# The low-part product of an attention logit, over 64 rows or over 128

## The chip, the cores and the metric

The kernel runs on one core of a Trainium2 chip. The metric is the device time of one execution in microseconds. Three runs of the kernel before took 2187.93, 2191.03 and 2192.39 us; their median, 2191.03 us, is the number that the prediction starts from.

## The reference, cut to what matters

The program is two transformer blocks, one after the other, on 512 tokens of width 1024, all in float32. Two places of it hold the products that the change touches: the selecting attention of the first block, with its scores and its logits, and the second attention of the second block.

```python
def dsa_attention(q, k, v, q_idx, k_idx, w_idx):     # first block, 4 blocks of 128 queries
    def block(args):
        raw = jnp.einsum('bqhd,bsd->bqhs', qib, k_idx) * idx_scale            # 8 heads of 64
        score = jnp.einsum('bqhs,bqh->bqs', jax.nn.relu(raw), wb)
        score = jnp.where(causal[None], score, -jnp.inf)
        _, sel = lax.top_k(score, k_top)                                      # 128 keys
        logits = jnp.einsum('bqhd,bqkd->bqhk', qb, k_sel) * attn_scale        # 8 heads of 64
        p = jax.nn.softmax(logits, axis=-1)
        return jnp.einsum('bqhk,bqkd->bqhd', p, v_sel)

def blocked_attention(q, k, v):                      # second block, 8 heads of 64, 2 of keys
    def one_block(qblk):
        s = jnp.einsum("bqhgd,bkhd->bhgqk", qblk, k)
        pr = jax.nn.softmax(s, axis=-1)
        return jnp.einsum("bhgqk,bkhd->bqhgd", pr, v)
```

## The kernel before, in words

Activations lie with features on partitions and tokens in the free dimension, 512 to a tile. TensorE takes float32r operands. So that products come out with float32 accuracy, each operand is a pair of tiles, a high part and a low part whose sum is the value, and a product of weights and activations is three matmuls (`mm3`, L283 to L285: high by high, high by low, low by high). Most of the program is streams of such products: for each output tile of 128 features a DMA brings 512 KB of weights, ScalarE casts the high part (L246), VectorE subtracts to get the low part (L247), and 24 matmuls of 512 columns follow.

The logits with heads of 64 features are made in another way, by `logits` (L629 to L636). A head has 64 rows only, so its tile of queries `q` (made in `heads`) holds the high part in 64 rows and the low part in the other 64. Keys (made in `keys`) come as two tiles: `hh` holds the high part in both halves of the rows, `ll` holds the low part in both halves. The first matmul (L635) multiplies all 128 rows of `q` with `hh`, which gives high by high plus low by high. The second (L636) multiplies the 64 rows of `q` with the high part by the 64 rows of `ll` beside them, which adds high by low, in the same bank of PSUM.

`logits` is called 88 times, at three places:

- **Scoring**, in `mix` (L790): 24 calls, 8 heads for each of three blocks of queries, with 256, 384 and 512 keys. ScalarE takes the result out of PSUM with a ReLU (L792), VectorE multiplies and adds it to the block's scores (L793). Then VectorE selects the best 128 keys of each query with 16 rounds of a maximum and a replacement (L804, L805), while TensorE goes on with the projections of the convolution's branch.
- **First attention**, in `mix` through `group` (L698): 32 calls, with 256 keys (16), 384 (8) and 512 (8). VectorE adds the bias and takes the maximum (L645), ScalarE exponentiates, VectorE scales.
- **Second attention**, in `mix2` through `group`: 32 calls with 512 keys. VectorE takes the maximum (L648).

In both attentions the weights of a group of four heads are transposed on TensorE (L670), split by ScalarE and VectorE (L672, L673), and multiplied with the values (L684, L685), one group behind the logits; products of the gates' weights stand between. The logits have three banks of PSUM ("lg"). Each engine works through its own list of instructions in order; the lists are made by the framework's scheduler from the order of the program and its own estimates.

Of the kernel before, what the change touches and what calls it, by code (L numbers as in the profile page):

```python
# [19 lines left out]
P = 128  # L20
# [18 lines left out]
# Columns of the array of per-feature vectors.  # L39
# [10 lines left out]
# Output tiles of w_in, in the order in which they are used.  # L50
T_KK, T_QI, T_VW, T_QA, T_CONV, T_GB, T_GA = 0, 1, 5, 6, 10, 22, 30
# Output tiles of w_in_2.
# [6 lines left out]
# How the work is cut and shared between the engines: P for GpSimd, V for VectorE, A for ScalarE.  # L59
# [116 lines left out]
class Net:  # L176
    def __init__(self, ctx, tc, a):
        self.tc, self.nc, self.a = tc, tc.nc, a
        pool = lambda name, bufs, **k: ctx.enter_context(tc.tile_pool(name=name, bufs=bufs, **k))  # noqa: E731
        self.cp = pool("cp", 1)  # L180
        self.xp = pool("xp", 16)
        self.slots = {t: pool(t + "p", n) for t, n in SLOTS.items()}
        self.sp = pool("sp", 2)
        self.wr = pool("wr", 2)
        self.wh = pool("wh", 5)
        self.wl = pool("wl", 5)
        # PSUM by use, so that each use goes on when another has to wait.
        self.banks = {t: pool(t, n, space=PSUM) for t, n in BANKS.items()}
        self.turn = 0
        self.attending = False  # L190
        self.spared = False
        self.sums = 0
        self.n = 0
        # What is still to be done before the stream h can be read: the rest of the last products,
        # and a post-norm's tiles and gain.
        self.rest = []
        self.due = None
        # The engine that takes the second parts of weights.
        self.second = self.nc.vector
        # The same for those between phases.  # L200
        self.lead = self.nc.vector

    # ---- tiles
# [22 lines left out]
    def pm(self):  # L226
        """For products; those of the attention's logits too while there are none."""
# [7 lines left out]
    # ---- products: each operand is a pair of float32r parts whose sum is the float32 value  # L235
    def load(self, src, shape):
        """The parts of weights; src and shape are [128, ...]."""
# [6 lines left out]
        view = lambda t: t.rearrange(f"p ({names}) -> p {names}", **{f"d{i}": v for i, v in enumerate(shape[1:])})  # noqa: E731  # L244
# [5 lines left out]
    def weights(self, w, n, nk, k0=0, count=1):  # L250
        """For each of count output tiles from n, the parts of its k-tiles."""
# [7 lines left out]
    def lead_weights(self, w, n, nk, k0=0, tag="b"):  # L259
        """The same for one output tile, in tiles that are free between phases."""  # L260
# [3 lines left out]
        # At the start the stream's input comes between the parts.  # L264
# [22 lines left out]
    def lin(self, wt, xs, tok=ALL, bank=None):  # L287
        """One output tile [128 features, tokens]."""
# [5 lines left out]
    def begin(self, jobs, step, fill=()):  # L294
        """The products of jobs by halves of the tokens, after the rest of the last phase's and after
        fill, with the steps of each half's norms between the products of the other half."""
# [24 lines left out]
        # A product is taken once its half's norm is there.  # L321
# [16 lines left out]
    def stream(self, jobs, tail=0, spare=0):  # L338
        """jobs: (weights, output tile, parts of the k-tiles, first k-tile, what takes the product).
        Of the last, the second half of the tokens is left to the next phase; some of these have weights in  # L340
        tiles of the norm's input that are free by then."""
# [9 lines left out]
    def split(self, src, parts, scale=None):  # L351
        """Writes the parts of src, or of src times a value per partition."""
# [14 lines left out]
    # ---- norms  # L367
# [6 lines left out]
    def rsqrt(self, v, tag, bufs=2):  # L374
        """x ** -0.5 of a small tile that has v = ROOT * x: from the exponent's bits, then by an iteration
        of the third order and one of the second, whose factors 1.5 and 2.25 are in ROOT."""
# [21 lines left out]
    def _sumsq(self, srcs, tag="sh"):  # L398
        """Tiles whose sum has, per partition and token, the sum of the squares of srcs."""
# [11 lines left out]
        # Sums of a few; the last goes into the product with ones at once.  # L411
# [9 lines left out]
    def rstd(self, accs, size, tag="r", bufs=4):  # L421
        """(mean + eps) ** -0.5, tokens on partitions: [128, tokens / 128]."""
# [11 lines left out]
    def row(self, r):  # L434
        """A value per token on every partition, in PSUM: [128, tokens]."""
# [6 lines left out]
    def rows(self, r, out):  # L442
        """The same in out."""
        self.nc.scalar.copy(out, self.row(r))
        return out
# [4 lines left out]
    def enter(self, gain, more=None):  # L450
        """The parts of h times the gain, the norm's factor per token for what is made of them, and
        the steps that compute both for a half of the tokens, after the post-norm that is due."""
# [44 lines left out]
    def leave(self, f, gain):  # L497
        """h += norm(f) * gain, when h is next needed."""
        self.due = f, gain

    # ---- parts of the net
    def setup(self):
        nc, a = self.nc, self.a
        c = lambda name, shape, dt=F32: self.cp.tile(shape, dt, tag=name, name=name)  # noqa: E731
# [4 lines left out]
        # The first activation brings the table of functions of the first part.  # L509
# [7 lines left out]
        # The stream's input, between the first weights.  # L517
# [5 lines left out]
        # The gains of the post-norms that the reference multiplies by a half.  # L523
# [12 lines left out]
    def down(self, w, f, k0, xs, add, late=(0, 0)):  # L536
        """f (+)= the product with the k-tiles of w from k0."""
# [47 lines left out]
    def rotated(self, w, n, xs, cos, sin, g=None, squares=None):  # L585
        """A job, and the tile that gets rope(its product, times a gain per row where there is one)."""
# [3 lines left out]
        def put(ps, tok):  # L590
            if squares is not None:
                nc.scalar.activation(squares[:, tok], ps, AF.Square)
            # y takes the 32-row blocks of each 64 rows exchanged.
# [12 lines left out]
    def heads(self, x):  # L606
        """Two heads of 64 rows: for each a tile with its hi part in its own rows, its lo part in the other's."""
# [10 lines left out]
    def keys(self, x, e):  # L618
        """The parts of the keys in rows 64e.. of x, each in both halves of a tile."""
# [9 lines left out]
    def logits(self, ps, q, e, i, keys, n):  # L629
        """[128 queries, n keys] of the head in tile q, whose hi part is in rows 64e.."""  # L630
        mm = self.nc.tensor.matmul
        own = slice(64 * e, 64 * e + 64)
# [3 lines left out]
        mm(ps[:, :n], lhsT=q[own, qs], rhs=ll[own, :n], start=False, stop=True)  # L636

    def softmax(self, ps, scale, n, bias=None, pool="V"):
        """Weights over n keys, for a scale that is positive (a number or a value per query)."""
# [24 lines left out]
    def turned(self, ps_, j):  # L664
        """The parts of the transposes of block j of the weights of some queries, side by side."""
# [10 lines left out]
    def pv(self, ps_, v):  # L676
        """sum over j of v[j].T @ (block j of the weights).T; v[j] has its hi part in columns 0-63,
        its lo part in the others."""
# [11 lines left out]
    def group(self, i, g, q, keys, v, ot, n, soft):  # L690
        """Four heads that share keys and values, for the queries of tile i, in two steps."""
        nc = self.nc
        ps = []
        for j in range(4):
            hd = 4 * g + j
            l = self.bank("lg")
            # Fewer than 256 columns would take longer.
# [10 lines left out]
    def overlapped(self, units):  # L708
        """Pairs of a generator of two steps and other work, each first step and the work before the
        second step of the unit before."""  # L710
# [12 lines left out]
    def values(self, ps, n):  # L723
        """[128 keys, hi | lo] of values whose transposes are in the columns of ps."""
# [6 lines left out]
    def projection(self, w, n, xs, r, alloc=None, light=False):  # L731
        """A job, and the tile that gets its product times r: on GpSimd where VectorE has much to do."""
# [18 lines left out]
    def mix(self):  # L751
# [28 lines left out]
        # The indexer's scores, and a bias that leaves each query its best keys.  # L780
# [28 lines left out]
        # The convolution's branch.  # L809
# [21 lines left out]
        # The attention, beside the other branch's gates.  # L831
# [26 lines left out]
    def gates(self, w, n, xs, r, count):  # L858
        """Tiles that get tanh(g / 2) of the gates g in some output tiles, one for each step of the
        generator; sigmoid(g) is (1 + tanh(g / 2)) / 2."""  # L860
# [25 lines left out]
    def branch(self, gates, w, xs, done=None):  # L886
        """gates = (gates + 1) * product of w and xs."""
# [7 lines left out]
    def merge(self, ga, gb, w, xb):  # L895
        """The parts of half the sum of ga and (gb + 1) * product of w and xb."""
# [9 lines left out]
    def memory_parts(self):  # L906
        """The parts of the normalised memory."""
# [12 lines left out]
    def memory(self):  # L920
        """Keys [features, M] by head, and values [M, features], of the memory, and what computes them."""
# [55 lines left out]
    def mix2(self):  # L977
# [19 lines left out]
        # The latents: the queries' norm factor goes into the softmax's scale.  # L997
# [11 lines left out]
        # The rotated part of the keys, in rows 64-95 of the tiles of keys.  # L1009
# [11 lines left out]
        # The first attention. Its values have keys on partitions, [hi | lo] of each head.  # L1021
# [21 lines left out]
        def prepare(hd):  # L1043
            """The parts of the queries of heads hd and hd + 1, and their keys and values."""
            # The first ones come before there are logits.
            bank = lambda: self.bank(K["pr"] if hd else "lg")
            if hd % 4 == 0:
                if hd == 0:
                    va.append(first_values(0))
                # The rotated parts of four heads: output tiles of them, and of the same exchanged.  # L1050
# [23 lines left out]
        # The second attention's heads: keys and queries without the norm's factor per token, which is  # L1074
        # in what their own norms' factors are.
        r2 = self.small("rsq", [P, NT], 1)
        nc.vector.scalar_tensor_tensor(r2, rt, 1.0 / 64, rt, op0=OP.mult, op1=OP.mult)
        wide = lambda t: t.unsqueeze(2).to_broadcast([P, NT, 2])  # noqa: E731
        two = lambda t: t.rearrange("p (t e) -> p t e", e=2)  # noqa: E731
# [95 lines left out]
    def mlp(self):  # L1175
# [14 lines left out]
        # The stream takes each part's product; the norm's input is kept in xs and r.  # L1190
# [43 lines left out]
    def final(self):  # L1234
# [3 lines left out]
        def step(tok):  # L1238
# [8 lines left out]
            def rows():  # L1247
                n = width(tok)
                outs = [self.tmp((P, 2 * n)).rearrange("p (k t) -> p k t", k=2) for _ in range(KD // 2)]
                # GpSimd takes some, whose gain ScalarE multiplies by before the norm's factor is there.  # L1250
# [45 lines left out]
# ---- layout of the inputs  # L1296
# [126 lines left out]
```

## Time and profile before

| | |
|---|---|
| runs | 2187.93, 2191.03, 2192.39 us (median 2191.03) |
| profiled execution, span of its instructions | 2187.6 us |
| TensorE matmuls, busy | 2125.2 us, 97% |
| TensorE weight loads, busy | 1754.7 us, 80% |
| VectorE, busy | 1290.8 us, 59% |
| ScalarE, busy | 910.1 us, 42% |
| GpSimd, busy | 307.5 us, 14% |
| granted clock of TensorE, mean | 0.984 of full |

The page gives no time for the profiled execution beside its span. The span is 0.3 us under the shortest of the three runs and 3.4 us under their median. A matmul's record is longer than what it costs: matmuls overlap, and their ends are modelled. What one costs is therefore read from the distance between the starts of neighbours, not from the length of a record. The granted clock is a share of 2.4 GHz; 0.5 is 1.2 GHz. In rows with "[x <-y]", the engine stood idle for x us before the instruction, and y ended that.

### The profile page before, as it was taken

The page shows a single profiled execution, that of the slowest core. Times are in us where ns is not written, and L with a number is a line of the kernel's source. Part 1 is how long each engine was busy: PE and PEld are TensorE (multiplying, and loading weights), DVE is VectorE, ACT ScalarE, POOL GpSimd, SP SyncE. Part 2 cuts the span into 40 slices and gives each one's busy share as a digit, 9 for nine tenths or more (in the row PEclk, how much of TensorE's full clock was granted, in tenths as well). Part 3 has the DMA queues.
Part 4 walks back from the last instruction along what each step waited for, and adds up shares of the span by engine and source line. Part 5 has one row for each costly group of instructions (what it writes and reads, how often), then busy time and mean ns, then how long its engine had stood idle before and what let it go on. Part 6 is the DMA issues. An engine that isn't in the chain of part 4 may idle for free.

```text
span 2187.6 us, 27792 instructions
## 1 busy us (share of the span) xinstructions
PE 2125.2 (97%) x10718; PEld 1754.7 (80%) x10718; DVE 1290.8 (59%) x2427; ACT 910.1 (42%) x1603; POOL 307.5 (14%) x275
## 2 busy tenths in 40 slices
PE   8999999899999989999999999998999999999997
PEld 7788888868777888898888888876667898888887
DVE  6344344869874685574243447678977663443565
ACT  5232223654464454452322224466764332222352
POOL 1101012303332120041010013122110000000011
PEclk9999999989999999999999999999999999999998
DMA  5233333203213234212333332211012322333331
GB/s 158 89 101 97 93 91 101 76 21 100 93 47 108 78 100 132 87 59 83 101 92 91 97 107 83 68 45 48 30 48 78 110 74 90 95 96 96 104 99 39
DMA packets 60229, 186.15 MB, mean 85 GB/s; under 512 B 6337, under 2 KB 13505, under 8 KB 60097
## 3 DMA queue, kind: packets, MB, share of 16 engines
q1 hardware_dynamic: 57616, 180.97, 27.1%
q10 hardware_dynamic: 2448, 3.41, 0.5%
q8 instruction: 84, 1.38, 0.3%
q14 instruction: 49, 0.39, 0.1%
q0 software_dynamic: 32, 0.00, 0.0%
HBM read 182.25 MB, written 2.10 MB: 84 GB/s over the span
## 4 chain that ended last, share of the span: by engine, by line
PE 84%; DVE 7%; issue 3%; ACT 2%; POOL 2%; DMA 2%; SPq 0%; POOLq 0%; ACTq 0%; DVEq 0%
PE mm L284 15%; PE mm L283 15%; PE mm L285 15%; PE lg L283 11%; PE lg L285 11%; PE lg L284 11%; DVE h L476 2%; PE lg L636 2%; PE tt L670 1%; PE lg L635 1%; DVE wl L247 1%; PE o L685 1%; PE o L684 1%; PE tt L428 1%; ACT wh L246 1%
## 5 line engine op out<-in xcount | busy, mean ns | idle before, releaser
L246 ACT CAST wh<-wr 128x1024 fp32r<-128x1024 f32 (+3 forms) x314 | 325.7, 1037 | 761.0 <-PE lg L284 344.8
L247 DVE TENSOR_TENSOR wl<-wr,wh 128x1024 fp32r<-128x1024 f32 (+2 forms) x312 | 415.9, 1333 | 150.2 <-ACT wh L246 146.9
L283 PE MATMUL mm<-x,wh 128*128 128x512 f32 (+1 forms) x1080 | 420.2, 389 | 0.0
L284 PE MATMUL mm<-x,wh 128*128 128x512 f32 (+1 forms) x1080 | 418.9, 388 | 0.0
L285 PE MATMUL mm<-x,wl 128*128 128x512 f32 (+1 forms) x1080 | 417.9, 387 | 0.0
L283 PEld LDWEIGHTS mm<-x,wh 128*128 128x128 f32 x1080 | 204.2, 189 | 46.0 <-issue 2.7
L284 PEld LDWEIGHTS mm<-x,wh 128*128 128x128 f32 x1080 | 204.3, 189 | 44.2 <-issue 2.4
L285 PEld LDWEIGHTS mm<-x,wl 128*128 128x128 f32 x1080 | 204.1, 189 | 44.2 <-issue 1.6
L283 PE MATMUL lg<-x,wh 128*128 128x512 f32 (+1 forms) x624 | 233.2, 374 | 0.0
L285 PE MATMUL lg<-x,wl 128*128 128x512 f32 (+1 forms) x624 | 233.2, 374 | 0.0
L284 PE MATMUL lg<-x,wh 128*128 128x512 f32 (+1 forms) x624 | 233.1, 374 | 0.0
L283 PE MATMUL mm<-b,wh 128*128 128x512 f32 (+1 forms) x493 | 175.6, 356 | 0.1
L284 PE MATMUL mm<-b,wh 128*128 128x512 f32 (+1 forms) x493 | 174.8, 355 | 0.4 <-DVE b L357 0.2
L285 PE MATMUL mm<-b,wl 128*128 128x512 f32 (+1 forms) x493 | 174.7, 354 | 0.0
L283 PE MATMUL lg<-b,wh 128*128 128x512 f32 (+1 forms) x455 | 161.8, 356 | 0.0
L285 PE MATMUL lg<-b,wl 128*128 128x512 f32 (+1 forms) x455 | 161.4, 355 | 0.0
L284 PE MATMUL lg<-b,wh 128*128 128x512 f32 (+1 forms) x455 | 161.3, 355 | 0.0
L565 POOL TENSOR_TENSOR t<-t,t 128x512 f32<-128x512 f32 (+1 forms) x48 | 66.3, 1382 | 579.5 <-ACT wh L246 486.7
L283 PEld LDWEIGHTS lg<-x,wh 128*128 128x128 f32 x624 | 117.6, 189 | 22.7
L285 PEld LDWEIGHTS lg<-x,wl 128*128 128x128 f32 x624 | 117.5, 188 | 22.7
L284 PEld LDWEIGHTS lg<-x,wh 128*128 128x128 f32 x624 | 117.6, 188 | 22.6
L356 ACT CAST b<-t 128x512 fp32r<-128x512 f32 (+1 forms) x100 | 58.8, 588 | 141.1 <-POOL t L565 68.0
(297 smaller groups left out, 3619.1 us busy)
## 6 DMA issues: line engine op xcount, KB each, us to landing
wr<-in_ffn_w SPq DMA_DIRECT2D x110, 512.0 KB, 3.6
wr<-in_w_in SPq DMA_DIRECT2D x64, 512.0 KB, 3.6
wr<-in_w_up SPq DMA_DIRECT2D x32, 512.0 KB, 3.6
wr<-in_w_down SPq DMA_DIRECT2D x32, 512.0 KB, 3.9
wr<-in_ffn_w SPq DMA_DIRECT2D x16, 448.0 KB, 3.4
wr<-in_w_out SPq DMA_DIRECT2D x8, 512.0 KB, 3.5
wr<-in_xattn_w_k SPq DMA_DIRECT2D x8, 512.0 KB, 3.7
wr<-in_xattn_w_v SPq DMA_DIRECT2D x8, 512.0 KB, 3.8
```

Source lines behind the costliest of these rows:

```text
L246: nc.scalar.copy(hi, raw)
L247: self.second.tensor_tensor(lo, raw, hi.bitcast(F32), op=OP.subtract)
L283: mm(ps, lhsT=a[0], rhs=b[0], start=first, stop=False)
L284: mm(ps, lhsT=a[0], rhs=b[1], start=False, stop=False)
L285: mm(ps, lhsT=a[1], rhs=b[0], start=False, stop=last)
L356: nc.scalar.copy(hi, src)
L428: nc.tensor.matmul(ps[:, i : i + 1], lhsT=acc[:, i * P : (i + 1) * P], rhs=self.ones, start=j == 0, stop=j == len(accs) - 1)
L476: nc.vector.scalar_tensor_tensor(h[k][:, tok], f, self.g(due[1], k), h[k][:, tok], op0=OP.mult, op1=OP.add)
L565: nc.gpsimd.tensor_tensor(t3[:, tok], t3[:, tok], t1[:, tok], op=OP.mult)
L635: mm(ps[:, :n], lhsT=q[:, qs], rhs=hh[:, :n], start=True, stop=False)
L636: mm(ps[:, :n], lhsT=q[own, qs], rhs=ll[own, :n], start=False, stop=True)
L670: nc.tensor.transpose(ps[:, b * P : b * P + P], p[:, j * P : j * P + P], self.ident)
```

## The change

The second matmul of `logits` takes all 128 rows of `q` and of `ll`. It thereby adds the product of the low parts, which the kernel before leaves out, and it addresses all rows of the array instead of the upper or the lower half.

```diff
     def logits(self, ps, q, e, i, keys, n):
         mm = self.nc.tensor.matmul
-        own = slice(64 * e, 64 * e + 64)
         qs = slice(i * P, i * P + P)
         hh, ll = keys
         mm(ps[:, :n], lhsT=q[:, qs], rhs=hh[:, :n], start=True, stop=False)
-        mm(ps[:, :n], lhsT=q[own, qs], rhs=ll[own, :n], start=False, stop=True)
+        mm(ps[:, :n], lhsT=q[:, qs], rhs=ll[:, :n], start=False, stop=True)
```

Nothing else of the program differs but comments. Both halves of `ll` and of `q` are written in the kernel before as well. The lists of the five engines hold the same instructions in the same order with the same waits; line numbers from `logits` on are one lower.

## Rows read from the trace of the kernel before

**Rows 1.** The page: span, and busy time of TensorE.

```profile
span 2187.6 us, 27792 instructions
PE 2125.2 (97%) x10718; PEld 1754.7 (80%) x10718; DVE 1290.8 (59%) x2427; ACT 910.1 (42%) x1603; POOL 307.5 (14%) x275
```

**Rows 2.** The chain that ended last, by engine.

```profile
PE 84%; DVE 7%; issue 3%; ACT 2%; POOL 2%; DMA 2%; SPq 0%; POOLq 0%; ACTq 0%; DVEq 0%
```

**Rows 3.** All instructions of L636: loads, matmuls, idle time before them (us, times).

```profile
L636 PEld LDWEIGHTS lg<-b,b x88: 182/183/286, 441.5 to 1643.1; 64*128 64x128 f32 x88
L636 PE MATMUL lg<-b,b x88: 378/492/687, 441.5 to 1643.1; 64*128 64x512 f32 x48, 64*128 64x256 f32 x24, 64*128 64x384 f32 x16
...
  issue: 20.9, 75
```

**Rows 4.** Timeline of TensorE's matmuls, second attention (start us, length us, instruction).

```profile
1612.41 0.39 PE L283 MATMUL mm<-x,wh 128*128 128x512 f32 x1
1612.64 0.40 PE L284 MATMUL mm<-x,wh 128*128 128x512 f32 x1
...
1617.16 0.40 PE L635 MATMUL lg<-b,b 128*128 128x512 f32 x1
1617.49 0.50 PE L636 MATMUL lg<-b,b 64*128 64x512 f32 x1
1617.91 0.51 PE L685 MATMUL o<-u,v 128*128 128x512 f32 x1
1618.26 0.60 PE L670 MATMUL tt<-ident,t 128*128 128x128 f32 x4
```

**Rows 5.** Timeline of TensorE's weight loads, the same stretch.

```profile
1612.41 0.19 PEld L284 LDWEIGHTS mm<-x,wh 128*128 128x128 f32 x1
...
1617.48 0.18 PEld L636 LDWEIGHTS lg<-b,b 64*128 64x128 f32 x1 [0.36 <-issue]
```

**Rows 6.** Timeline of matmuls, first attention: four pairs of 256 keys.

```profile
588.05 0.28 PE L635 MATMUL lg<-b,b 128*128 128x256 f32 x1
...
590.45 0.50 PE L283 MATMUL mm<-x,wh 128*128 128x512 f32 x1
```

**Rows 7.** Timeline of matmuls: products over 96 rows, in the second block's other attention.

```profile
1536.87 0.40 PE L284 MATMUL lg<-b,b 96*128 96x512 f32 x1
1537.11 0.40 PE L285 MATMUL lg<-b,b 96*128 96x512 f32 x1
```

**Rows 8.** Timeline of matmuls, scoring: the first, two in its midst, and the first behind it.

```profile
441.16 0.39 PE L635 MATMUL lg<-b,b 128*128 128x256 f32 x1 [2.86 <-DVE b L614]
...
446.55 0.63 PE L285 MATMUL mm<-x,wl 128*128 128x512 f32 x1
446.98 0.63 PE L283 MATMUL mm<-x,wh 128*128 128x512 f32 x1
...
474.14 0.50 PE L283 MATMUL mm<-x,wh 128*128 128x512 f32 x1
```

**Rows 9.** Stretches: length; busy us of PE, PEld, DVE, ACT, POOL; PEclk; DMA.

```profile
393.80:397.20 3.40, 3.34 (x15) 3.35 (x16) 3.40 (x9) 2.43 (x7) 0.00 (x0) 0.51 0.42 139
441.60:462.10 20.50, 20.50 (x46) 12.56 (x46) 11.19 (x25) 7.93 (x20) 0.00 (x0) 0.50 0.09 26
462.10:474.10 12.00, 12.00 (x34) 5.70 (x32) 8.46 (x17) 7.36 (x13) 0.00 (x0) 1.00 0.00 0
474.10:578.80 104.70, 104.70 (x450) 84.51 (x450) 98.28 (x191) 45.77 (x66) 34.68 (x23) 1.00 0.29 88
580.00:643.00 63.00, 62.80 (x264) 43.91 (x263) 42.80 (x171) 40.34 (x94) 17.87 (x14) 1.00 0.17 51
1541.00:1643.20 102.20, 100.73 (x444) 69.75 (x443) 85.72 (x230) 72.39 (x139) 11.12 (x8) 1.00 0.12 37
```

**Rows 10.** ScalarE's ReLUs of scoring: shortest, median, longest (ns).

```profile
L792 ACT ACTIVATE t<-lg x24: 383/490/601, 445.4 to 474.2; 128x256 f32<-128x256 f32 x8, 128x384 f32<-128x384 f32 x8, 128x512 f32<-128x512 f32 x8
```

**Rows 11.** VectorE's longest wait in 1541 to 1643.2 (us, times, longest).

```profile
DVE u L673 <- ACT u L672: 7.0, 12, 1.3
```

## The prediction

> **What bounds the kernel now.** I read the page first. TensorE has matmuls under way in 2125.2 us of the span of 2187.6 us, and the chain that ended last runs over it for 84% [rows 1, 2]. So time that TensorE gains comes off the end, wherever no other engine is close behind it. But a busy share says nothing of whether the matmuls stand as close as they could. So I went to the line that changes, L636 [rows 3]: 88 matmuls, 48 of 512 columns, 24 of 256 and 16 of 384. Their weight loads have an idle time before them, 20.9 us in 75 cases, which is put down to "issue": they wait for nothing that the profile shows.
>
> The timeline tells what that is. A product of 512 columns over all rows starts 0.23 us after the one before it (1612.41 to 1612.64). From L635 to L636 it is 0.33 us (1617.16 to 1617.49), from L636 to the next matmul 0.42 (to 1617.91), and from that to its successor still 0.35 (to 1618.26) [rows 4]. The loads show why: the load for a product over all rows runs beside the matmul before it (L284's load starts at 1612.41, its matmul at 1612.64), while L636's load has waited 0.36 us and starts only with its own matmul [rows 4, 5]. My reading: TensorE lets everything run out when it goes from all rows to half of them, and again on the way back.
>
> Is it the number of rows, or that L636 adds to a bank and closes it? The other attention has triples of products that also add up in one bank, over 96 rows. They stand 0.24 us apart [rows 7]. So 96 rows count as a full array, and adding up costs nothing.
>
> Then I asked of each stretch who is next behind TensorE [rows 9]. In the first attention VectorE is busy 42.80 of 63.00 us and ScalarE 40.34: much room. In the second, VectorE is busy 85.72 of 102.20 us: little. In scoring the granted clock is 0.50 from 441.6 to 462.1, that is 1.2 GHz. Ahead of it TensorE had stood 2.86 us for VectorE [rows 8]. Behind scoring comes the selection, in which VectorE is busy 98.28 of 104.70 us [rows 9].
>
> **The change part by part.** Nothing is moved on any queue, and no wait is added. What changes is what 88 pairs cost.
>
> *One product.* The three distances in the second attention add up to 1618.26 - 1617.16 = 1.10 us; three plain ones are 3 x 0.233 = 0.70 (0.233 is the 0.23 of rows 4 over many products). Gain: 0.40 us. In the first attention four pairs of 256 columns take 590.45 - 588.05 = 2.40 us [rows 6] where eight plain products of half the columns take 8 x 0.117 = 0.94; with 0.10 for the product behind them as in rows 4, the gain is (2.40 - 0.94 + 0.10) / 4 = 0.39 us. The width hardly matters, so I take 0.40 us everywhere at full clock. What the 64 further rows may cost: a load takes 183 ns over 64 rows and 0.19 us over 128 [rows 3, 5], and both lie beside a matmul. I cost it at nothing; without that cover it is 88 x 7 ns = 0.6 us.
>
> *First attention:* 32 x 0.40 = 12.8 us. VectorE and ScalarE leave 20 us of room, so all of it counts. Lower bound 10, if a fifth goes to waits for results.
>
> *Second attention:* 32 x 0.40 = 12.8 us. VectorE's work with its longest wait, for ScalarE's split of the transposed weights [rows 11], is 85.72 + 7.0 = 92.7 us of 102.2. That leaves 9.5 us, and I take 9.5. Upper bound 12.8, since those waits begin with transposes on TensorE that come sooner too; lower bound 5, half of what I take, if other waits in these chains stay as they are.
>
> *Scoring.* It runs from 441.16 to 474.14, 33.0 us for 79 matmuls [rows 8]: the 24 pairs, 27 products of 512 columns for weights, 4 small transposes. Plainly spaced at full clock they take 43 x 0.233 + 16 x 0.175 + 16 x 0.117 = 14.7 us (43 of 512 columns, 16 each of 384 and 256, counted by their columns). At half clock a product of 512 columns takes 0.43 us (446.55 to 446.98) [rows 8], and all of it 27.0 us. So much hangs on when the clock rises. If it stays at half until 462.1 as now, 20.9 us do 77% of the work, the rest takes 3.3 us, and the stretch is 24.3 us: 8.7 gained. But another stretch at half clock, behind a pause of TensorE near 390 us, was only some 3.4 us long, with weight products on TensorE and no 64-row product among them [rows 9]. With products that stand without gaps from 441.16 on I expect the same here. Then 14.7 + 1.7 = 16.4 us, about 17.4 with a wait or two for banks: 15.6 gained. Can the others follow? ScalarE's work in these 32.5 us is 7.93 + 7.36 = 15.3 us, in which the 24 ReLUs take 8 x (0.38 + 0.49 + 0.60) = 11.8 [rows 9, 10]. VectorE's work there is 11.19 + 8.46 = 19.65, so it can come at most 12.85 us sooner [rows 9]. Since the selection behind it keeps VectorE nearly full, VectorE's lead is what lasts: I take 13 us, between the bounds 8.7 and 15.6.
>
> *A rule that speaks against the change.* Rows 4 show a full-array product on either side of the 64-row one. The Trainium skill, "TensorEngine Tiling (Array Packing)", section Overview, gives up to twice the speed for contractions of 64 rows or less, with tiles that work in parallel. By it, two 64-row products side by side would cost one, and giving up half the rows would lose up to 8 us as an estimate from the page's factor. No row here has two such products as neighbours, so I put that at zero.
>
> *Sum:* 12.8 + 9.5 + 13 = 35.3 us; with all lower bounds 23.7, with all upper ones 41.2. The profiled execution's span, 2187.6 us, would become 2152.3. The median of the runs is 3.4 us above that span; I take the saving from the median: 2191.0 - 35.3 = 2155.7, say 2156, with 2149.8 to 2167.3 as this case's own bounds.
>
> **The rivals.**
>
> *A: VectorE hands the scoring's gain back.* The selection behind scoring leaves VectorE 6.4 us free in 104.7 [rows 9]. If it doesn't start sooner, TensorE stands at the three banks of the first attention, and of scoring's gain nothing is left; with the lower bounds of both attentions, 15 us are gained: 2176. Against it: in scoring VectorE is idle 12.85 of 32.5 us, and those idle times end when TensorE delivers.
>
> *B: it is not the rows.* If the gaps belong to any second product of a pair with the same queries, nothing changes but at most 0.6 us of loads: 2191. Against it stand the triples of 96 rows [rows 7].
>
> *C, slower: the load no longer goes beside the matmul.* L636 would then use the same rows as L635, and its load could be held until L635 has run out. At 512 columns it would start 0.40 + 0.19 = 0.59 us after L635 [rows 4, 5] instead of 0.33, with 256 columns 0.28 + 0.19 = 0.47 instead of 0.30 on average (2.40 us over eight) [rows 6]. With the 384s counted as the 256s and the gaps behind L636 left as they are, that costs 48 x 0.26 + 40 x 0.17 = 19.3 us: 2210. It decides if the new load starts after L635's end. Against it: L284's load starts with the matmul of L283 and uses the same rows [rows 4, 5]. The Trainium skill, "TensorE: Matmul & The Clock Gate", Part 3, says that a load overlaps a matmul under way only when the row group differs, which is this rival; the rows just named differ from it.
>
> **How the numbers follow.** My case has 80%, A 12%, B 5%, C 3%. The range takes in my case's bounds, opens downward by 3 us for the scatter of runs (they lie 4.5 us apart), and upward toward A to 2173, for a smaller gain in scoring: 2147 to 2173. Some 0.2%, 4.4 us, is what a measurement can tell from no change. My case and A are faster by more: 92%. B is the same: 5%. C is slower: 3%.
>
> **What would show it.** In the profile after, the loads of the second product start one matmul ahead, and their 20.9 us of idle time are gone. The second product starts 0.23 us after the first at 512 columns, and so does the next. The granted clock is back at 1.00 well before 462 us. The first matmul behind scoring starts near 459 us, the first attention's first pair, now near 580, stands some 13 us sooner, and the second attention is 9 to 10 us shorter. It is wrong if the distances stay at 0.33 and 0.42 (B), if they grow (C), or if TensorE has new waits for VectorE ahead of the first attention (A).

## The result, and the profile after

The changed kernel takes 2155.85 us (median of 4 runs, 2151.55 to 2159.54), the kernel before 2191.71 us (4 runs, 2187.93 to 2193.28). The ratio is 0.9841 with a 95% interval of 0.9824 to 0.9857: 35.9 us less. In a later series of runs the same kernel took 2155.55 us against 2187.25 (ratio 0.9857, 0.9842 to 0.9871), 31.7 us less. The two medians of the kernel before differ by 4.5 us, so the gain is 32 to 36 us.

The page after, its span, busy times and chain:

```profile
span 2149.4 us, 27792 instructions
PE 2083.3 (97%) x10718; PEld 1741.7 (81%) x10718; DVE 1287.4 (60%) x2427; ACT 907.5 (42%) x1603; POOL 309.2 (14%) x275
...
PE 78%; DVE 11%; issue 4%; ACT 3%; DMA 2%; POOL 2%; SPq 0%; POOLq 0%; ACTq 0%; DVEq 0%
```

TensorE's busy share is 97% as before [rows 1]. That share did not see the gaps, and it does not see that they are gone: a matmul's record simply ends sooner. In the chain that ended last TensorE has 78% where it had 84%, VectorE 11% where it had 7% [rows 2].

The instructions of the second product (now L635), after, shortest, median and longest in ns:

```profile
L635 PEld LDWEIGHTS lg<-b,b x88: 187/189/338, 439.5 to 1606.1; 128*128 128x128 f32 x88
L635 PE MATMUL lg<-b,b x88: 274/392/481, 439.6 to 1606.3; 128*128 128x512 f32 x48, 128*128 128x256 f32 x24, 128*128 128x384 f32 x16
```

A load takes 189 ns in the median (183 before), and the list of idle times in front of it, 20.9 us in 75 cases before [rows 3], is empty. The matmuls of the second attention, after (start, length):

```profile
1583.00 0.48 PE L634 MATMUL lg<-b,b 128*128 128x512 f32 x1
1583.32 0.40 PE L635 MATMUL lg<-b,b 128*128 128x512 f32 x1
1583.56 0.48 PE L683 MATMUL o<-u,v 128*128 128x512 f32 x1
1583.87 0.39 PE L634 MATMUL lg<-b,b 128*128 128x512 f32 x1
1584.10 0.39 PE L635 MATMUL lg<-b,b 128*128 128x512 f32 x1
1584.33 0.45 PE L684 MATMUL o<-u,v 128*128 128x512 f32 x1
1584.61 0.60 PE L669 MATMUL tt<-ident,t 128*128 128x128 f32 x4
```

and the loads of the second of these pairs:

```profile
1583.65 0.19 PEld L634 LDWEIGHTS lg<-b,b 128*128 128x128 f32 x1
1583.88 0.19 PEld L635 LDWEIGHTS lg<-b,b 128*128 128x128 f32 x1
```

The pair at 1583.87 is the one of rows 4. Its three distances were 0.33, 0.42 and 0.35 us; they are 0.23, 0.23 and 0.28. L635's load begins at 1583.88, with the matmul of L634, and is there when its own matmul starts at 1584.10. Before, it began with its own matmul [rows 5]. The 0.32 us at 1583.00 is no gap of the change: behind transposes the first product takes that long with full products only, too.

Where the time went is read from the starts of the same instruction in both traces. Before, beside those of rows 8:

```profile
579.94 0.28 PE L635 MATMUL lg<-b,b 128*128 128x256 f32 x1
...
646.53 0.33 PE L670 MATMUL tt<-ident,t 128*128 128x128 f32 x1
...
1540.62 0.48 PE L635 MATMUL lg<-b,b 128*128 128x512 f32 x1
...
1643.50 0.50 PE L685 MATMUL o<-u,v 128*128 128x512 f32 x1
```

After, the same six instructions, those of scoring first:

```profile
439.41 0.39 PE L634 MATMUL lg<-b,b 128*128 128x256 f32 x1 [2.85 <-DVE b L614]
...
456.78 0.39 PE L283 MATMUL mm<-x,wh 128*128 128x512 f32 x1
...
562.48 0.28 PE L634 MATMUL lg<-b,b 128*128 128x256 f32 x1
...
620.17 0.27 PE L669 MATMUL tt<-ident,t 128*128 128x128 f32 x1
...
1511.89 0.48 PE L634 MATMUL lg<-b,b 128*128 128x512 f32 x1
...
1606.57 0.39 PE L684 MATMUL o<-u,v 128*128 128x512 f32 x1
```

| stretch | lead at its start, us | lead at its end, us | gained, us | forecast, us |
|---|---|---|---|---|
| scoring | 1.75 | 17.36 | 15.6 | 13 (8.7 to 15.6) |
| selection | 17.36 | 17.46 | 0.1 | 0 |
| first attention | 17.46 | 26.36 | 8.9 | 12.8 (10 to 12.8) |
| second attention | 28.73 | 36.93 | 8.2 | 9.5 (5 to 12.8) |

The three stretches gain 32.7 us. The other 5.5 us of the two spans' 38.2 (1.75 ahead of scoring, 0.1 in the selection, 2.4 between the attentions, 1.3 behind) lie where the change does nothing. The profiled execution is also the shortest of the four, 2151.55 us. Such parts differ between executions of one kernel too: in another profile of the changed kernel (`e11_change_again`) scoring began 2.3 us later than in the kernel before, not 1.75 sooner.

The stretches of rows 9, after (columns as there):

```profile
440.20:443.60 3.40, 3.40 (x12) 2.81 (x13) 3.27 (x5) 2.41 (x8) 0.00 (x0) 0.50 0.00 0
443.60:458.60 15.00, 15.00 (x75) 12.43 (x74) 14.61 (x36) 12.83 (x29) 0.00 (x0) 1.00 0.12 35
458.60:561.40 102.80, 102.80 (x442) 82.80 (x441) 99.35 (x194) 44.25 (x64) 35.17 (x23) 1.00 0.30 89
562.40:617.00 54.60, 52.30 (x265) 42.42 (x264) 41.91 (x170) 40.12 (x94) 17.84 (x14) 1.00 0.19 59
1511.90:1606.50 94.60, 91.86 (x447) 69.49 (x445) 84.95 (x232) 72.08 (x138) 10.78 (x8) 1.00 0.13 40
```

The clock is at half for 3.4 us of scoring instead of 20.5. In the second attention VectorE is now busy 84.95 of 94.60 us, 90%.

### The profile page after: what moved, and what is told of

Same layout as the page of the kernel before. It is cut to its first block, busy times and chain, and to the rows that moved or that the text cites. A ratio compares the mean times of both kernels' runs of the same rounds, so it can differ in the third digit from the quotient of the medians.

```text
span 2149.4 us, 27792 instructions
## 1 busy us (share of the span) xinstructions
PE 2083.3 (97%) x10718; PEld 1741.7 (81%) x10718; DVE 1287.4 (60%) x2427; ACT 907.5 (42%) x1603; POOL 309.2 (14%) x275
## 4 chain that ended last, share of the span: by engine, by line
PE 78%; DVE 11%; issue 4%; ACT 3%; DMA 2%; POOL 2%; SPq 0%; POOLq 0%; ACTq 0%; DVEq 0%
PE mm L284 13%; PE mm L283 13%; PE mm L285 13%; PE lg L283 11%; PE lg L284 11%; PE lg L285 11%; DVE wl L247 2%; DVE h L476 2%; PE tt L669 1%; DVE b L804 1%; DVE m L803 1%; PE o L684 1%; PE o L683 1%; ACT wh L246 1%; PE tt L428 1%
```

## The experiments

The first six runs in this part only set over which rows a product runs. Five of them leave every engine's list of instructions and its order as they were. In `e5_both_64_rows` TensorE's records stand in another order at two places, one in scoring and one in the second attention.

**One part alone.** In `e1_scoring_only` the 24 pairs of scoring have the change, in `e2_attentions_only` the 64 pairs of the attentions.

```diff
-        mm(ps[:, :n], lhsT=q[:, qs], rhs=ll[:, :n], start=False, stop=True)
+        r = slice(0, P) if full else slice(64 * e, 64 * e + 64)
+        mm(ps[:, :n], lhsT=q[r, qs], rhs=ll[r, :n], start=False, stop=True)
```

`full` is an argument that is true at the one call (scoring) or at the other (`group`).

> Full rows in the 24 pairs of scoring only; the 64 pairs of both attentions keep 64 rows. Theory (gaps at the change of rows, and a granted clock that comes back sooner): scoring shrinks by 15.6 us as in the changed kernel, the selection hands nothing back, 2191.7 - 15.6 = 2176. Rival (VectorE's selection hands the lead back before the first attention): under 5 us gained, 2187 or more.

> Full rows in the 64 pairs of both attentions only. Theory: 8.9 + 8.3 = 17.2 us gained as the changed kernel's trace has it there, 2174.5; scoring stays at 33 us with the clock at 0.5 for some 20 us of it. If the attentions lost something only because scoring had come sooner (VectorE behind), they gain more here, up to 11.5 + 11.9 = 23 us, 2168.

Measured: 2173.65 us with scoring alone (ratio 0.9925, 0.9909 to 0.9941) and 2172.03 us with the attentions alone (0.9918, 0.9903 to 0.9933), beside 2190.63 us before. By the medians that is 17.0 and 18.6 us, together 35.6, as much as both in one kernel. In the traces scoring gains 14.6 us in the first; the attentions gain 9.3 and 8.3 us in the second, where scoring stays as it was. So it is not scoring's coming sooner that keeps the first attention at 8.9 us: with scoring as it was, it gains hardly more. The selection hands nothing back: the first attention begins as much sooner as scoring ended.

**When the clock comes back.** Two runs have the change in one part of scoring only: `i == 1` in place of `full` (the first 8 pairs), and `i > 1` (the last 16).

> Full rows in the first 8 pairs of scoring (256 keys) only. Theory (products without gaps bring the clock back): clock back at 1.0 after some 3.4 us, the 16 later pairs then cost 0.40 us each at full clock; scoring 33.0 - (15.7 - 6.4) = 23.7 us, total 2182.4. Rival (only the gaps of these 8 pairs count, the clock comes back when it did): 8 x 0.6 = 5 us gained, clock at 0.5 until about 460, total 2187.

> Full rows in the last 16 pairs of scoring (384 and 512 keys) only. Theory: the clock stays at 0.5 through the first 8 pairs, to about 454, and comes back some 3.4 us behind them, sooner than 462; scoring shrinks by 9 us, total 2183. Rival (the clock comes back at about 462 whatever the pairs do): 6.6 us, total 2185.

Measured: 2181.24 us (0.9963, 0.9952 to 0.9974; 12 runs from 2178.28 to 2187.16) and 2183.28 us (0.9966, 0.9955 to 0.9978). The clock in the run with the first 8 pairs:

```profile
440.90:447.70 6.80, 6.37 (x21) 5.28 (x22) 6.52 (x14) 5.56 (x13) 0.00 (x0) 0.50 0.00 0
447.70:464.70 17.00, 17.00 (x58) 9.50 (x56) 13.36 (x30) 9.89 (x21) 0.00 (x0) 1.00 0.10 31
464.70:471.50 6.80, 6.80 (x15) 4.70 (x15) 2.52 (x4) 3.55 (x6) 1.28 (x1) 0.50 0.00 0
```

Full pairs at the start bring the clock back at 447.7, 6.8 us after it fell, where it stayed down for 20.5 us before [rows 9]. Nothing else was changed, so the pairs with gaps were what held it down, and the theory stands. But the third row was not foreseen: with the 64-row pairs of 512 keys it fell again at 464.7, without any pause of TensorE, to which the profile gives 17.00 of 17.00 us of busy time. Such pairs don't always bring it down: in the kernel before they ran from 466.4 to 474.1 at 1.00 [rows 9]. What decides is not shown. In the other run the clock is down for 17.1 us and rises 5.4 us after the last 64-row product, which starts at 453.7:

```profile
442.00:459.10 17.10, 17.10 (x43) 11.91 (x43) 10.15 (x24) 7.37 (x19) 0.00 (x0) 0.50 0.10 31
459.10:467.00 7.90, 7.90 (x38) 6.33 (x37) 6.64 (x14) 6.55 (x14) 0.00 (x0) 1.00 0.00 0
```

Its time does not tell the theory (2183) from the rival (2185). Nor does the clock: it came back 3.4 us sooner after its fall than in the kernel before, and two profiles of the changed kernel differ by as much (3.4 and 6.8 us, `e11_change_again`).

**Is a 64-row product slow by itself, or the change of rows?** In `e5_both_64_rows` the first product of a pair runs over the 64 rows with the high part as well.

```diff
-        mm(ps[:, :n], lhsT=q[:, qs], rhs=hh[:, :n], start=True, stop=False)
+        mm(ps[:, :n], lhsT=q[own, qs], rhs=hh[own, :n], start=True, stop=False)
```

> The first product of each pair takes only the 64 rows with the high part too (low by high is left out), the second stays at 64 rows, so both products of a pair use the same half. Theory (the cost sits where the number of rows changes): no gap within a pair nor between neighbouring pairs; four neighbouring pairs of 256 keys take 8 x 0.117 + about 0.4 = 1.3 us instead of 2.4; a lone pair still costs 0.4 us more than a full one. In time scoring some 8, first attention 7, second attention 4 us sooner: 2172. Rival (a 64-row product costs some 0.2 us more by itself): twice as many of them, four pairs take 2.4 us or more, total 2191 or more. Second rival (neighbours in different halves run side by side): four pairs take under 0.94 us.

Measured: 2174.15 us beside 2188.78 before (0.9931, 0.9907 to 0.9954). Three neighbouring pairs of the first attention, in the order of their start; x2 is two matmuls merged:

```profile
579.21 0.39 PE L635 MATMUL lg<-b,b 64*128 64x256 f32 x2
579.43 0.28 PE L636 MATMUL lg<-b,b 64*128 64x256 f32 x2
579.55 0.28 PE L635 MATMUL lg<-b,b 64*128 64x256 f32 x1
579.67 0.28 PE L636 MATMUL lg<-b,b 64*128 64x256 f32 x1
```

So the first rival is out: among its like a 64-row product starts 0.12 us after the one before it, as a full one of 256 columns does (579.55 to 579.67). The theory holds for these, though not for the first pair behind a full product, whose second product starts 0.22 us after its first. The second rival holds in part. Two products of heads in opposite halves, in two banks, take the time of one: the two of 579.43 take 0.12 us, and the six start within 0.46 us, where the kernel before has two products in 0.60 (four pairs in 2.40 [rows 6]). The time came out as forecast, but not its parts. By the trace scoring and the pause ahead of it gained 10.6 us, the first attention 1.9 and the second 0.3. In the second the pairs stand alone between full products and pay as before. In the first they were early at the three banks and waited, and the clock fell for 3.4 us at 571.5. This run also bears on another reading of the clock, that half an array of rows, and not the gaps, holds it down. With all 48 products of scoring over 64 rows it was down there for 6.9 and 3.4 us, less than the 20.5 before, which speaks against that reading. But the run's pauses differ too, so it doesn't rule it out.

**96 rows.** In `e6_96_rows` the second product of the heads in the upper 64 rows runs over 96 rows.

```diff
-        mm(ps[:, :n], lhsT=q[:, qs], rhs=ll[:, :n], start=False, stop=True)
+        r = slice(0, P) if e else slice(0, 96)
+        mm(ps[:, :n], lhsT=q[r, qs], rhs=ll[r, :n], start=False, stop=True)
```

> The second product of the heads in the upper 64 rows takes 96 rows, that of the others 128; part of low by low is thereby added. Theory (96 rows are a full array): the time of the change, 2156, starts 0.117 us apart at 256 columns. Rival (anything short of 128 rows pays): 44 of 88 pairs pay 0.40 us, 2173.

Measured: 2155.92 us beside 2188.78 before (0.9846, 0.9821 to 0.9871), the time of the change. The first attention's first products there:

```profile
565.31 0.28 PE L634 MATMUL lg<-b,b 128*128 128x256 f32 x1
565.43 0.28 PE L636 MATMUL lg<-b,b 96*128 96x256 f32 x1
565.54 0.28 PE L634 MATMUL lg<-b,b 128*128 128x256 f32 x1
```

0.12 and 0.11 us apart: 96 rows go with 128, without a gap.

**The pause ahead of scoring.** Four runs put products that nobody reads into TensorE's pause ahead of scoring, in both kernels, 10 of them or 20:

```diff
         ka, ki = self.keys(kk, 0), self.keys(kk, 1)
+        o = self.bank("o")
+        for _ in range(10):
+            nc.tensor.matmul(o, lhsT=ki[0][:, :P], rhs=ki[0], start=True, stop=True)
```

> The kernel before, with 10 products of 512 columns that nobody reads in TensorE's pause ahead of scoring (2.9 us). Theory A (only the pause brought the clock down): clock 1.0 through scoring, which takes 14.7 + 24 x 0.40 = 24.3 us, 8.7 us gained, 2182. Theory B (the gaps of the 64-row pairs bring it down by themselves, as they did a second time at 464.7 us in the run with the first block only): the clock is down for 7 us or more within scoring, 0 to 5 us gained.

> The changed kernel with the same 10 products in the pause ahead of scoring. If the pause alone brings the clock down there, it stays at 1.0 and 1.7 us are gained: 2154. If the fall comes all the same, nothing: 2156.

> The kernel before with 20 instead of 10 products that nobody reads ahead of scoring, so that TensorE hardly pauses there. Theory B (the gaps of the 64-row pairs bring the clock down by themselves): a stretch at 0.5 begins within scoring all the same, and less than 5 us are gained. Theory A (the pause alone): clock 1.0 from 438 to 474, some 8 us gained.

> The changed kernel with the same 20 products. Both theories: clock 1.0 through scoring, since neither pause nor gaps are left; 1.7 us gained over the change where nothing else moves, so 1 to 3 us under its run in this call.

> The changed kernel once more, beside the one with 20 filling products: 2156, within the scatter of some 4 us either way that its first runs had.

Measured: before with 10, 2189.53 us (1.0003, 0.9989 to 1.0017); change with 10, 2154.64 us (0.9844, 0.9821 to 0.9867); before with 20, 2198.93 us (1.0051, 1.0036 to 1.0066); change with 20, 2163.00 us (0.9885, 0.9868 to 0.9901), beside 2155.55 us for the change in the same series. None of them does what it was made for. The scheduler put two small transposes and more pairs ahead of the first product for weights, and TensorE then paused elsewhere, for 2.2 us behind the 10 products and for 2.0 to 2.4 us behind the first four pairs with 20. So whether the fall goes away without any pause was not tried. The change with 20 is 7.5 us slower, where 1 to 3 us less were expected. In part that may be the 4.7 us from the first of the 20 products to the end of the last; the rest I did not follow.

But the two runs with 20 have the same lists and nearly the same pause, and the clock fell at about the same place. The first of these rows are the kernel before with 20:

```profile
443.10:447.20 4.10, 3.10 (x11) 1.72 (x11) 3.94 (x6) 2.82 (x8) 0.00 (x0) 1.00 0.00 0
447.20:477.90 30.70, 29.72 (x52) 14.45 (x53) 17.53 (x40) 10.61 (x22) 0.00 (x0) 0.50 0.06 17
```

and these are the change with 20:

```profile
448.50:451.90 3.40, 3.40 (x15) 3.30 (x14) 2.21 (x9) 2.27 (x7) 0.00 (x0) 0.50 0.49 154
451.90:461.00 9.10, 9.10 (x42) 7.10 (x41) 9.10 (x18) 7.03 (x15) 0.00 (x0) 1.00 0.00 0
```

Once fallen, the clock stayed at half for 30.7 us with 64-row pairs, and for 3.4 us with full ones. The two runs with 10 have the same lists as each other too, and there it was 13.6 and 3.4 us.

## Why the prediction was right, and where it was not

The forecast was 2156 us, and the runs gave 2155.85 and 2155.55. The total is closer than its terms, which were off in both directions. That it came so close is in part luck.

- **The gaps come with the change of rows.** Right. The distances and the loads after are as forecast, and among its like a 64-row product has no gap (`e5_both_64_rows`). Rival B is out by `e6_96_rows` and by the result. Rival C is out: the load of L635 starts with the matmul ahead of it, over the same rows. The rule that the rival rests on, from the Trainium skill, "TensorE: Matmul & The Clock Gate", Part 3, is not what these rows show.
- **The tiles' speed-up.** The rule of "TensorEngine Tiling (Array Packing)" in the Trainium skill, section Key Properties, that different tiles can load and multiply in parallel, does hold in `e5_both_64_rows`: two products start within 0.01 us of each other in its x2 rows above. It was rightly priced at zero here, since in the kernel before each 64-row product stands between full ones.
- **First attention, 12.8 us with "all of it counts" and a lower bound of 10.** This term failed: 8.9 us in the profile, 9.3 with the attentions alone. Two things were missed. The 0.40 us were taken at pairs with full products on both sides; a pair that has transposes behind it gains less. Such a pair with its transposes, before:

```profile
626.84 0.42 PE L635 MATMUL lg<-b,b 128*128 128x384 f32 x1
...
627.87 0.48 PE L284 MATMUL mm<-x,wh 128*128 128x512 f32 x1
```

and after:

```profile
603.63 0.42 PE L634 MATMUL lg<-b,b 128*128 128x384 f32 x1
...
604.31 0.48 PE L284 MATMUL mm<-x,wh 128*128 128x512 f32 x1
```

That is 1.03 and 0.68 us, 0.35 less. And free time of VectorE in sum does not mean that it is free when asked. After, TensorE stops at the fourth pair, and once more behind the pairs:

```profile
564.56 0.39 PE L634 MATMUL lg<-b,b 128*128 128x256 f32 x1 [1.21 <-DVE sm_m L644]
...
597.07 0.50 PE L683 MATMUL o<-u,v 128*128 128x512 f32 x1 [1.01 <-ACT u L671]
```

VectorE at the first of these times:

```profile
561.00 0.43 DVE L805 TENSOR_SCALAR b<-b 128x512 f32<-128x512 f32 x1
563.07 1.23 DVE L247 TENSOR_TENSOR wl<-wr,wh 128x1024 fp32r<-128x1024 f32 x1 [1.64 <-ACT wh L246]
564.21 0.28 DVE L644 CUSTOM_DVE_ANT_0 t<-lg,first 128x128 f32<-128x128 f32 x1
```

It has nothing to do for 1.64 us, because a low part of weights stands ahead of the logits' maximum in its list and waits for ScalarE's cast. The three banks fill and TensorE waits. VectorE's wait was there before as well, but the slower pairs hid it from TensorE:

```profile
580.17 1.23 DVE L247 TENSOR_TENSOR wl<-wr,wh 128x1024 fp32r<-128x1024 f32 x1 [1.39 <-ACT wh L246]
```

The second wait is for ScalarE's part of the split weights; before, it was 0.20 us. With what the two waits grew by added back, 8.9 + 1.21 + 0.81 = 10.9 us, the 32 pairs have 0.34 us each.

- **Second attention, 9.5 us.** 8.2 measured, so the term was 1.3 us too large. That VectorE's load was the limit is not shown: TensorE's waits in this stretch grew from 1.0 us to 2.6, of which 0.5 for VectorE and 1.1 for ScalarE. The rest of what is missing from 12.8 us lies in distances that shrank by less than 0.40 us for a pair, as in the first attention. So the size of this term came near for a reason that the trace doesn't bear out.
- **Scoring, 13 us, "VectorE's lead is what lasts".** It gave 15.6, which was the upper bound from TensorE's side. VectorE finished the selection at 561.00 + 0.43 instead of 17.36 us later. Before:

```profile
477.28 0.69 DVE L598 TENSOR_TENSOR t<-mm,b 128x512 f32<-128x512 f32 x1 [3.70 <-ACT t L596]
...
578.36 0.43 DVE L806 TENSOR_SCALAR b<-b 128x512 f32<-128x512 f32 x1
```

The sum of VectorE's idle time, 12.85 us, was cut off at 474.1. Of the 3.70 us of idle time that ended at 477.28, 3.2 lay behind that cut, and after the change the wait at this place is 0.48 us. Rival A is out: no engine handed anything back before the first attention.

- **The clock.** Right in kind: pairs without gaps bring it back. In the profile of the result it took 3.4 us, as forecast; with the change in scoring alone and in the second profile of the change, 6.8 us, and scoring then gained 14.6 us.

Together the three terms were 3.9 and 1.3 us too large and 2.6 us too small, which leaves them 2.6 us above the 32.7 us that the trace has.

## What to carry to other kernels

A matmul over half of the rows in the midst of full ones is dearer than one over all rows: 0.34 to 0.40 us each here at full clock, although it multiplies half as much. If the other half of the tile holds anything that may be added, run it over all rows. Zeros there should do as well, but no run tried them. Or keep 64-row products together, in opposite halves and in different banks; here that alone, without a new order of the program, came to 2174 us, and full rows to 2156. Read TensorE from the distances between starts, since its busy share was 97% with the gaps and without them.

## What the runs showed that I had not expected

The granted clock fell without a pause of TensorE. In the run with the first 8 pairs changed it went from 1.00 to 0.50 at 464.7 us, while 64-row pairs of 512 keys ran and the profile has TensorE busy all the time. Gaps of 0.1 to 0.2 us that are in no list of TensorE's waits for others thus cost twice in scoring: directly, and by the clock. In scoring both together were 15.6 us for 24 pairs, 0.65 us each, against 0.26 to 0.28 (8.2 and 8.9 us for 32) in the attentions, where the clock stayed at 1.00.
